# Two pieces of a loaded ahead of b's first slices, in a matmul–GELU–matmul kernel

## The chip, the cores and the metric

The kernel runs on one core of a Trainium2 chip. The metric is the time of one execution on the device in microseconds (us), the median of several runs. Beside it there is one execution taken with the hardware profiler.

## What is computed

```python
m, k, n, p = 1024, 1024, 2048, 1024          # a: m x k, b: k x n, c: n x p, all float32
h = np.matmul(a, b)
h = 0.5 * h * (1 + np.tanh(np.sqrt(2 / np.pi) * (h + 0.044715 * h ** 3)))
return np.matmul(h, c).astype(np.float32)
```

## The kernel before

The order of every engine's instructions is written out by hand, in the order of the program's text; no planner moves anything. TensorE computes h transposed, 128 rows of n at a time ("tiles" t), in two halves h of 512 rows of m. All of it is accumulated in eight PSUM banks of 128 x 512.

The first 512 columns of b (tiles 0 to 3) are done plainly: for each slice k of 128 along the contraction, `block(h, tiles, (k,))` issues one matmul per tile into the bank of that tile, with b's slice (128 x 128 of it) as weights and 512 columns of a transposed, `aT[:, h, k]`, as the moving operand. The rest of b and the whole second matmul are done in the manner of Strassen, as seven products instead of eight (`seven(zero…)`, `seven(one…)`, `seven(two…)`), with sums on VectorE. They come after the plain part and are not touched, but for how one output tile is stored.

a must be transposed, and that too is TensorE's work. It is loaded in eight pieces (h, q): half h, quarter q of the contraction, 512 x 256, 512 KB in float32. A piece is brought to bf16 (`cast_a`, on VectorE and ScalarE) and then turned: `turn(h, q, banks, ab)` is a generator that in each of two steps issues four transposes of 128 x 128 into a PSUM bank and one VectorE copy to `aT`. Each step gives one slice k = 2q + n. The program takes a step with `next(tn)` and puts matmuls between.

Loads come on two queues:

- SP's queue carries float32 pieces, which are then cast on the engines: a(0,0), b's slices 0 and 1 (one load of 512 KB, "b's first pair"), a(1,0), a(0,1), and b's slice 2 (256 KB). They go to `sta` and `stb`, and `cast_b(k, engines…)` splits the cast of one slice of b by columns among the engines named.
- GpSimd's queue carries everything else and casts to bf16 on the way (`abq`, `b1`, `b2`, `c_sb`). It is held back by `gate`, a copy on GpSimd that waits for a(0,0). Its order is a(1,1), b's slice 3, then for q = 2 and 3 a(0,q), b's slices 2q and 2q+1, a(1,q), and after them the rest of b and c. The first eight loads are issued one after the other; each further one waits until the load eight places ahead of it has landed.

`stir(widths…)` issues matmuls of zeros of the given widths, whose result nobody reads; each is a float32 matmul, which the trace shows as two. `make_identity` on GpSimd makes the identity matrix that the transposes multiply with; the first transpose waits for GpSimd, and that includes the gate copy.

The order of TensorE at the head, before the change, is: five stirs of 256; four transposes of a(0,0); stir 128; four transposes of a(0,0); stir 64; `block(0, range(4), (0,))` and `block(0, range(2), (1,))`, six matmuls; the eight transposes of a(1,0); two more matmuls of half 0 and three of half 1; four transposes of a(0,1); three matmuls of half 1; four transposes; and then a loop over q = 1, 2 with blocks of four and three matmuls and four transposes in turn. It ends with a(1,3), the last piece.

In the profile, L114 are the matmuls of `block`, L145 the transposes, L146 the copies to `aT`, L110 the casts on VectorE and L108 those on ScalarE, L125 the stirs, L75 to L79 SP's loads, L81 the gate, L86 and L89 and L92 GpSimd's first loads of a and b, L98 the loads of b's columns 512 to 1023, L212 the matmuls of the seven products, L429 the stores. The changed kernel is four lines shorter, so its numbers are lower by one (L80 to L199) or four (from about L290).

Of the kernel before, what the change touches and what calls it, by code (L numbers as in the profile page):

```python
# [19 lines left out]
def kernel(ctx, tc, a, b, c, out):  # L20
    nc = tc.nc
    M, K = a.shape
    _, N = b.shape
    _, P = c.shape
    H = 512
# [4 lines left out]
    bv = b.rearrange("(kt p) n -> p kt n", p=128)  # L30
# [9 lines left out]
    def slot(tag, shape, dt, name):  # L40
        return big.tile(shape, dt, name=name, tag=tag)

    def bank(i, shape=(128, H), dt=F32, name="ps"):
        return pp.tile(list(shape), dt, name=name, tag=f"bank{i}", padded_shape=None)

    def pieces(tag, bufs, shape, dt, name):
        return small.tile(shape, dt, name=name, tag=tag, bufs=bufs)
# [12 lines left out]
    b1 = slot("b1", [128, KT, 1024], BF16, "b1")  # L60
# [4 lines left out]
    stb = slot("x0", [128, KT, H], F32, "stb")  # L65
    sta = slot("x1", [128, 2, 2, 4, 256], F32, "sta")
    abq = slot("x3", [128, 4, 2, 4, 256], BF16, "abq")

    def a_part(h, q):
        return av[:, 4 * h:4 * h + 4, ds(q * 256, 256)]  # L70

    def b_part(q):
        return bv[:, 2 * q:2 * q + 2, 0:H]

    nc.sync.dma_start(out=sta[:, 0, 0], in_=a_part(0, 0))  # L75
    nc.sync.dma_start(out=stb[:, 0:2], in_=b_part(0))
    nc.sync.dma_start(out=sta[:, 1, 0], in_=a_part(1, 0))
    nc.sync.dma_start(out=sta[:, 0, 1], in_=a_part(0, 1))
    nc.sync.dma_start(out=stb[:, 2], in_=bv[:, 2, 0:H])  # L79

    nc.gpsimd.tensor_copy(gate, sta[:, 0, 0, 3, 0:1])  # L81
    nc.scalar.activation(g, warm[:, 0:1], AF.Gelu_apprx_tanh)
# [2 lines left out]
    def cast_load_a(h, q):  # L85
        nc.gpsimd.dma_start(out=abq[:, q, h], in_=a_part(h, q))  # L86

    def cast_load_b(q):
        nc.gpsimd.dma_start(out=b1[:, 2 * q:2 * q + 2, 0:H], in_=b_part(q))  # L89

    cast_load_a(1, 1)
    nc.gpsimd.dma_start(out=b1[:, 3, 0:H], in_=bv[:, 3, 0:H])  # L92
    for q in range(2, 4):
        cast_load_a(0, q)
        cast_load_b(q)
# [3 lines left out]
    for n in range(2):  # L99
        for k in range(0, KT, 4):  # L100
            nc.gpsimd.dma_start(out=b2[:, k:k + 4, ts(n, H)],
                                in_=bv[:, k:k + 4, ds(1024 + n * H, H)])
# [3 lines left out]
    def copy(eng, dst, src):  # L106
        if eng is nc.scalar:
            nc.scalar.activation(dst, src, AF.Copy)  # L108
        else:
            nc.vector.tensor_copy(dst, src)  # L110

    def mm1(p, t, h, ks):
        for k in ks:
            nc.tensor.matmul(p, b1[:, k, ts(t, 128)], aT[:, h, k],  # L114
                             start=(k == 0), stop=(k == KT - 1))
# [6 lines left out]
    def stir(*widths):  # L122

        for w in widths:
            nc.tensor.matmul(ps[0, 3][:, 0:w], warm[:, 0:128], warm[:, 0:w],  # L125
                             start=True, stop=True, skip_group_check=True)

    def cast_a(h, q, *engs):

        ab = pieces("ab", 2, [128, 4, 256], BF16, "ab")  # L130
        for i, eng in enumerate(engs):
            w = 256 // len(engs)
            for j, e in enumerate(eng if isinstance(eng, tuple) else (eng,)):
                m = slice(2 * j, 2 * j + 2) if isinstance(eng, tuple) else slice(0, 4)
                copy(e, ab[:, m, ts(i, w)], sta[:, h, q][:, m, ts(i, w)])
        return ab

    def turn(h, q, i, ab):

        banks = i if isinstance(i, tuple) else (i,)  # L140
        pts = [bank(x, (128, 2, H), BF16, "pt") for x in banks]
        for n in range(2):
            pt = pts[n % len(pts)]
            for m in range(4):
                nc.tensor.transpose(pt[:, n, ts(m, 128)], ab[:, m, ts(n, 128)], ident)  # L145
            nc.vector.tensor_copy(aT[:, h, 2 * q + n], pt[:, n])  # L146
            yield

    def cast_b(k, *engs):
        c0 = 0  # L150
        for i, eng in enumerate(engs):
            w = (H - c0) if i == len(engs) - 1 else H // len(engs) // 128 * 128
            copy(eng, b1[:, k, ds(c0, w)], stb[:, k, ds(c0, w)])
            c0 += w

    def block(h, tiles, ks):
        for k in ks:
            for t in tiles:
                mm1(ps[h, t], t, h, (k,))
# [56 lines left out]
    def pair(i):  # L216
        x = slot(f"x{i}", [128, 2, 4, H], F32R, "x1")
        return x[:, 0], x[:, 1]
# [8 lines left out]
    one = Seven(4, quarters(b2, 0, H), BB, [None] * 4, zero.t)  # L227

    stir(256, 256, 256, 256, 256)
    tn = turn(0, 0, 4, cast_a(0, 0, nc.vector))  # L230
    next(tn)
    stir(128)
    cast_b(0, nc.vector, nc.vector, nc.scalar)
    next(tn)
    stir(64)
    cast_b(1, nc.scalar)
    ab = cast_a(1, 0, nc.vector, nc.scalar)
    block(0, range(4), (0,))
    block(0, range(2), (1,))
    for _ in turn(1, 0, (7, 6), ab):  # L240
        pass
    block(0, range(2, 4), (1,))
    ab = cast_a(0, 1, (nc.scalar, nc.vector), nc.vector)
    cast_b(2, nc.scalar, nc.scalar)
    for t in range(3):
        ps[1, t] = bank(4 + t)
    zero.t[0], zero.t[1] = pair(2)
    block(1, range(3), (0,))
    tn = turn(0, 1, 7, ab)
    next(tn)  # L250
    block(1, range(3), (1,))
# [2 lines left out]
    for q in range(1, 3):  # L254
        k = 2 * q
        block(0, range(4), (k,))
        tn = turn(1, q, 7, abq[:, q, 1])
# [5 lines left out]
        tn = turn(0, q + 1, 7, abq[:, q + 1, 0])  # L263
# [10 lines left out]
    tn = turn(1, 3, 0, abq[:, 3, 1])  # L274
# [153 lines left out]
    def store(mt, q0, w, ot, eng=None):  # L428
        (eng or nc.sync).dma_start(out=out[ts(mt, 128), ds(q0, w)], in_=ot)  # L429

    def done2(i, l, j, p):
        if (i, l) == (1, 0):
            ot = pieces("o", 4, [128, H], F32, "ot")
            nc.vector.tensor_copy(ot, p)
            p = ot
        n = 2 if (i, l, j) == (0, 0, 1) else 1
        for q in range(n):
            r = ds(q * (H // n), H // n)
            store(4 * i + j, l * H + q * (H // n), H // n, p[:, r])

    def between2(n):
# [12 lines left out]
        elif n == "P73":  # L454
            two.t4(two.t[1], 4)

    seven(two, done2, between2)


# [28 lines left out]
```

## Time and profile before

| | us |
|---|---|
| median of 3 runs | 117.21 (117.09 to 117.56) |
| the profiled execution | 117.6 |
| its span, first to last record | 115.8 |
| TensorE busy with matmuls in the span | 110.7 (96%) |
| VectorE, ScalarE, GpSimd busy | 90.1, 51.4, 17.3 |
| first load issued, first transpose, first matmul of h | 0.74, 5.21, 6.90 |
| last matmul group ends, last VectorE instruction starts | 112.9, 112.93 |

The span is shorter than the execution by 1.8 us, which lie ahead of the first and behind the last record. Lines of a timeline or of a chain begin with the start and the length in us; "x4" means four instructions merged into one line; in square brackets stands how long the engine was idle before it and what ended that. A matmul's own length includes the time until its result is out, so that the next may start before it ends. "To landing" is the time from the start of a load's issue until the last of its parts has arrived.

### The profile page before, as it was taken

Reading aid. Unit: us, or ns where it says so; the run is one execution under the profiler, and the core shown is the slowest. Engines: PE = TensorE matmul, PEld = TensorE weight load, DVE = VectorE, ACT = ScalarE, POOL = GpSimd, SP = SyncE. Lnnn points to the kernel's source line nnn. Section 1 sums busy time; section 2 is a strip of 40 time slices with the busy share of each in tenths; the row PEclk is TensorE's granted clock in tenths of the full one; section 3 lists DMA queues with packets and bytes.
Section 4 is the critical chain, followed back from the end, with each engine's and each line's share of the span. In section 5 each row is a group of like instructions: output and inputs, shape, how many; then the busy total and the mean of one; then the engine's idle time right before and its main releaser. Section 6 shows DMA issues by size and latency. Waiting matters only on the chain.

```text
span 115.8 us, 1473 instructions
## 1 busy us (share of the span) xinstructions
PE 110.7 (96%) x544; PEld 77.1 (67%) x550; DVE 90.1 (78%) x108; ACT 51.4 (44%) x86; POOL 17.3 (15%) x29
## 2 busy tenths in 40 slices
PE   7889999999999999999999999999999999999990
PEld 6545555445777447888886444588888888888870
DVE  0247747689999998944789999999999986964581
ACT  5053000799268998066699339700043992000000
POOL 2497754222332000000000000000000000000000
PEclk9999999999999999999999999999999999999999
DMA  3999999999999999998000000070000002004994
GB/s 74 296 381 221 200 199 204 204 207 207 205 210 210 211 212 212 212 210 163 9 0 0 6 0 0 0 272 0 0 0 0 0 0 94 2 27 173 364 358 166
DMA packets 13414, 15.94 MB, mean 138 GB/s; under 512 B 736, under 2 KB 9184, under 8 KB 13408
## 3 DMA queue, kind: packets, MB, share of 16 engines
q0 software_dynamic: 8672, 9.31, 47.6%
q1 hardware_dynamic: 4592, 6.42, 15.7%
q10 hardware_dynamic: 144, 0.13, 0.3%
q8 instruction: 4, 0.07, 0.2%
q14 instruction: 2, 0.02, 0.0%
HBM read 20.97 MB, written 4.19 MB: 217 GB/s over the span
## 4 chain that ended last, share of the span: by engine, by line
PE 79%; DMA 13%; POOL 5%; issue 0%; DVE 0%
PE ps L212 76%; DMA abq<-in_a_dram 10%; DMA sta<-in_a_dram 3%; POOL abq L86 3%; PE ps L114 2%; POOL b L89 1%; POOL gate L81 1%; PE pt L145 1%; POOL b L92 0%; DVE ot L375 0%
## 5 line engine op out<-in xcount | busy, mean ns | idle before, releaser
L212 PE MATMUL ps<-x,s 128*128 128x512 f32 x128 | 29.6, 391 | 0.0
L212 PEld LDWEIGHTS ps<-x,s 128*128 128x128 f32 x128 | 24.0, 188 | 5.1
L212 PE MATMUL ps<-x,x 128*128 128x512 f32 x96 | 22.9, 394 | 0.0
L212 PEld LDWEIGHTS ps<-x,x 128*128 128x128 f32 x96 | 18.0, 188 | 3.9
L114 PE MATMUL ps<-aT,b 128*128 128x512 bf16 x62 | 15.7, 379 | 0.3 <-DVE b L110 0.2
L298 ACT ACTIVATE v<-ps 128x512 f32<-128x512 f32 x10 | 6.0, 598 | 19.1 <-PE ps L212 19.1
L212 PE MATMUL ps<-c_sb,hT 128*128 128x512 bf16 (+2 forms) x78 | 14.1, 336 | 0.1
L212 PE MATMUL ps<-x 128*128 128x512 f32 x56 | 13.2, 393 | 0.0
L212 PEld LDWEIGHTS ps<-x 128*128 128x128 f32 x56 | 10.2, 188 | 2.7 <-ACT u L298 0.4
L212 PEld LDWEIGHTS <-hT 128*128 128x128 bf16 x80 | 7.1, 98 | 7.0 <-issue 0.5
L118 ACT ACTIVATE hT<-ps 128x512 bf16<-128x512 f32 x14 | 7.3, 596 | 9.6 <-PE ps L114 9.6
L118 ACT ACTIVATE hT<-ot 128x512 bf16<-128x512 f32 x18 | 10.4, 623 | 2.1 <-DVE ot L303 2.0
L146 DVE COPY aT<-pt 128x512 bf16<-128x512 bf16 x16 | 6.7, 422 | 5.5 <-PE pt L145 5.4
L212 PE MATMUL ps<-aT,b 128*128 128x512 bf16 x46 | 10.6, 379 | 0.1
L303 DVE TENSOR_TENSOR ot<-ps,u 128x512 f32<-128x512 f32 x10 | 6.7, 688 | 5.2 <-ACT u L298 5.2
L303 DVE TENSOR_TENSOR ot<-ps,v 128x512 f32<-128x512 f32 x10 | 6.7, 688 | 4.9 <-DMA out_dram<-ot 3.9
L170 DVE TENSOR_TENSOR x<-c_sb 128x1024 fp32r<-128x1024 bf16 x8 | 9.2, 1216 | 0.0
L114 PEld LDWEIGHTS <-b 128*128 128x128 bf16 x64 | 5.7, 97 | 4.5 <-DVE b L110 0.3
L212 PEld LDWEIGHTS <-b 128*128 128x128 bf16 x48 | 4.6, 97 | 5.7 <-issue 0.3
L104 POOL DMA_DIRECT2D c_sb<-in_c_dram x8 | 5.6, 703 | 13.4 <-DMA b<-in_b_dram 11.1
L170 DVE TENSOR_TENSOR x<-b 128x1024 fp32r<-128x1024 bf16 (+1 forms) x4 | 7.0, 1751 | 0.6 <-issue 0.6
L298 ACT ACTIVATE u<-ps 128x512 f32<-128x512 f32 x10 | 5.9, 597 | 3.4 <-PE ps L212 3.2
(44 smaller groups left out, 110.7 us busy)
## 6 DMA issues: line engine op xcount, KB each, us to landing
c_sb<-in_c_dram POOLq DMA_DIRECT2D x8, 512.0 KB, 19.7
out_dram<-ot SPq DMA_DIRECT2D x14, 256.0 KB, 2.1
b<-in_b_dram POOLq DMA_DIRECT2D x6, 512.0 KB, 15.6
sta<-in_a_dram SPq DMA_DIRECT2D x3, 512.0 KB, 6.2
abq<-in_a_dram POOLq DMA_DIRECT2D x5, 256.0 KB, 8.0
stb<-in_b_dram SPq DMA_DIRECT2D x1, 512.0 KB, 5.4
b<-in_b_dram POOLq DMA_DIRECT2D x2, 256.0 KB, 8.3
stb<-in_b_dram SPq DMA_DIRECT2D x1, 256.0 KB, 7.2
```

The source lines that it names most:

```text
L81: nc.gpsimd.tensor_copy(gate, sta[:, 0, 0, 3, 0:1])
L86: nc.gpsimd.dma_start(out=abq[:, q, h], in_=a_part(h, q))
L89: nc.gpsimd.dma_start(out=b1[:, 2 * q:2 * q + 2, 0:H], in_=b_part(q))
L104: nc.gpsimd.dma_start(out=c_sb[:, t:t + 2], in_=cv[:, t:t + 2])
L114: nc.tensor.matmul(p, b1[:, k, ts(t, 128)], aT[:, h, k], start=(k == 0), stop=(k == KT - 1))
L118: nc.scalar.activation(hT[h][:, t], p, AF.Gelu_apprx_tanh)
L145: nc.tensor.transpose(pt[:, n, ts(m, 128)], ab[:, m, ts(n, 128)], ident)
L146: nc.vector.tensor_copy(aT[:, h, 2 * q + n], pt[:, n])
L170: nc.vector.tensor_tensor(out=dst[:, r], in0=x[:, r], in1=y[:, r], op=op)
L212: nc.tensor.matmul(p[:, ds(c0, w)], l[:, k, ts(j, 128)], r[:, k, ds(c0, w)], start=(start and k == 0), stop=(k == self.kt - 1), skip_group ...
L298: nc.scalar.activation(st, p, AF.Copy)
L303: nc.vector.tensor_tensor(out=ot, in0=p, in1=st, op=ADD)
```

## The change

SP's queue loads a(1,0) ahead of b's first pair, and no longer loads b's slice 2. GpSimd's queue loads b's slices 2 and 3 together, in first place, ahead of a(1,1). a(0,0) is cast half on VectorE and half on ScalarE, and its two steps of transposes go to two banks, one straight after the other. After them come the eight transposes of a(1,0), with stirs of 256 and 64 ahead of them and one of 128 behind them, and only then matmuls: four of slice 0 for half 0, three of slice 0 for half 1, four of slice 1 for half 0. These are the same eleven that stood ahead of a(0,1)'s transposes before; from these on the order is the old one. In `cast_b(0, …)` ScalarE takes the first 256 columns as two of 128 and VectorE the last 256 (before, VectorE took the first 256 and ScalarE the last). One more output tile is stored in two halves.

```diff
     nc.sync.dma_start(out=sta[:, 0, 0], in_=a_part(0, 0))
+    nc.sync.dma_start(out=sta[:, 1, 0], in_=a_part(1, 0))
     nc.sync.dma_start(out=stb[:, 0:2], in_=b_part(0))
-    nc.sync.dma_start(out=sta[:, 1, 0], in_=a_part(1, 0))
     nc.sync.dma_start(out=sta[:, 0, 1], in_=a_part(0, 1))
-    nc.sync.dma_start(out=stb[:, 2], in_=bv[:, 2, 0:H])
...
+    cast_load_b(1)
     cast_load_a(1, 1)
-    nc.gpsimd.dma_start(out=b1[:, 3, 0:H], in_=bv[:, 3, 0:H])
...
     stir(256, 256, 256, 256, 256)
-    tn = turn(0, 0, 4, cast_a(0, 0, nc.vector))
-    next(tn)
+    for _ in turn(0, 0, (4, 5), cast_a(0, 0, nc.vector, nc.scalar)):
+        pass
+    stir(256, 64)
+    tn = turn(1, 0, (7, 6), cast_a(1, 0, nc.scalar, nc.vector))
+    next(tn)
+    cast_b(0, nc.scalar, nc.scalar, nc.vector)
+    next(tn)
+    cast_b(1, nc.scalar)
     stir(128)
-    cast_b(0, nc.vector, nc.vector, nc.scalar)
-    next(tn)
-    stir(64)
-    cast_b(1, nc.scalar)
-    ab = cast_a(1, 0, nc.vector, nc.scalar)
-    block(0, range(4), (0,))
-    block(0, range(2), (1,))
-    for _ in turn(1, 0, (7, 6), ab):
-        pass
-    block(0, range(2, 4), (1,))
-    ab = cast_a(0, 1, (nc.scalar, nc.vector), nc.vector)
-    cast_b(2, nc.scalar, nc.scalar)
     for t in range(3):
         ps[1, t] = bank(4 + t)
+    block(0, range(4), (0,))
+    block(1, range(3), (0,))
+    block(0, range(4), (1,))
+    ab = cast_a(0, 1, (nc.scalar, nc.vector), nc.vector)
     zero.t[0], zero.t[1] = pair(2)
-    block(1, range(3), (0,))
     tn = turn(0, 1, 7, ab)
...
-        n = 2 if (i, l, j) == (0, 0, 1) else 1
+        n = 2 if (i, l) == (0, 0) and j else 1
```

## The prediction

> **What bounds the kernel now.** I read the page first: busy shares, then the chain.
>
> ```profile
> PE 110.7 (96%) x544; PEld 77.1 (67%) x550; DVE 90.1 (78%) x108; ACT 51.4 (44%) x86; POOL 17.3 (15%) x29
> ...
> PE ps L212 76%; DMA abq<-in_a_dram 10%; DMA sta<-in_a_dram 3%; POOL abq L86 3%; PE ps L114 2%; POOL b L89 1%; POOL gate L81 1%; PE pt L145 1%; POOL b L92 0%; DVE ot L375 0%
> ```
>
> TensorE is the bound, and 4% of a span of 115.8 is all that is left to it. The change touches the first 11 us only (and one store), so the question is what a shift of TensorE's early work does to its last matmul. The chain in order of time says where TensorE last waited for something from outside:
>
> ```profile
> 10.15 11.43 DMA abq<-in_a_dram
> 21.58 0.05 issue
> 21.63 0.40 PE pt L145 x4
> ```
>
> The last a piece, a(1,3), lands at 21.58; its four transposes start 0.05 later. After that the chain is TensorE's own to 112.93. The timeline of TensorE shows the head:
>
> ```profile
> 5.21 0.40 PE L145 MATMUL pt<-ident,ab 128*128 128x128 bf16 x4 [0.42 <-POOL gate L81]
> ...
> 6.90 1.47 PE L114 MATMUL ps<-aT,b 128*128 128x512 bf16 x6 [0.17 <-DVE b L110]
> 8.47 0.62 PE L145 MATMUL pt<-ident,ab 128*128 128x128 bf16 x8
> 8.93 1.26 PE L114 MATMUL ps<-aT,b 128*128 128x512 bf16 x5
> 10.03 0.39 PE L145 MATMUL pt<-ident,ab 128*128 128x128 bf16 x4
> ...
> 19.16 2.32 PE L114 MATMUL ps<-aT,b 128*128 128x512 bf16 x10
> 21.63 0.40 PE L145 MATMUL pt<-ident,abq 128*128 128x128 bf16 x4
> ```
>
> Ten matmuls take 2.32 with the last one's 0.38, so one follows another after (2.32 - 0.38)/9 = 0.216. The ten end their turn at 19.16 + 10 x 0.216 = 21.32, and the next start is 21.63: TensorE stands idle 0.31 there, for a(1,3). From 10.03 to 21.32 it is full; the windows view gives the same:
>
> ```profile
> 8.40:10.00 1.60, 1.53 (x13) 0.90 (x14) 1.11 (x5) 0.64 (x2) 1.60 (x3) 1.00 1.20 275
> 10.00:21.30 11.30, 11.20 (x80) 6.09 (x81) 7.83 (x16) 1.58 (x4) 6.12 (x9) 1.00 1.35 201
> 21.30:21.70 0.40, 0.26 (x3) 0.08 (x3) 0.22 (x1) 0.40 (x2) 0.00 (x0) 1.00 1.25 205
> 21.70:112.90 91.20, 90.98 (x424) 65.45 (x428) 78.44 (x82) 45.91 (x76) 4.93 (x7) 1.00 0.53 116
> ```
>
> (The first number after each stretch is its length, the next TensorE's busy time, and the 1.00 after the engines is the granted clock.) So two times carry everything: when TensorE reaches the four transposes of a(0,1), at 10.03, with 11 matmuls and 16 transposes behind it; and 21.58. In the changed order the same 11 matmuls and 16 transposes stand ahead of these four transposes, and from there on TensorE's order is the old one. The end moves by (change of 10.03) - 0.31, as long as a(1,3) is no later, and no load between becomes late.
>
> **The change part by part.**
>
> *SP's queue.* Landing times, from issue start plus "to landing" of each load: a(0,0) 0.74 + 3.7 = 4.44; b's pair 1.22 + 5.4 = 6.6; a(1,0) 1.77 + 6.2 = 7.97; a(0,1) 2.27 + 7.1 = 9.4; b's third slice 2.82 + 7.2 = 10.0. They land in the order of issue, so the queue is one pipe: 512 KB took 2.15 (b's pair), then 1.38 and 1.4 (the a pieces). The change swaps second and third. The three first loads are the same bytes, so b's pair now lands when the third load did: 7.97. Ends: if the slowness of the second load (2.15 against 1.38) is gone in the new order, 4.44 + 2 x 1.38 = 7.20; if a(1,0) as the second and b's pair as b each pay it, 4.44 + 2 x 2.15 = 8.74. I take 7.97, because the slowness stays in the sum whether it goes with the place or with the tensor. a(1,0) lands between 5.8 and 6.6. a(0,1) stays at 9.4, and SP issues one load less.
>
> *First matmul.* Before, b's pair landed at 6.6 and the first matmul ran at 6.90, after a 128-wide VectorE cast of 0.22. Now the first 128 columns are ScalarE's. Its casts of b took 0.40 at 256 wide and 0.61 at 512, so 128 wide is about 0.29, and the first matmul comes 0.40 after the landing: 8.37. ScalarE's second 128 (0.2 to 0.29 more) is ready for the second matmul at 8.59; VectorE's 256 columns (0.3) are in time for the third. Slice 1 is one ScalarE cast of 0.61, done by 9.2, and needed at the eighth matmul, 8.37 + 7 x 0.216 = 9.9. The 11 matmuls, now without a gap, end at 8.37 + 11 x 0.216 = 10.74. a(0,1), landed at 9.4, is cast by 9.9 to 10.3 (ScalarE is free at 9.2), so its transposes start at 10.74, against 10.03: **0.71 later**.
>
> *All turns first.* The eight transposes of a(0,0) start together at 5.21 (they wait for the gate copy as before), those of a(1,0) at about 6.5 to 7.3 (landing plus a ScalarE cast of 0.63). They cost nothing: TensorE has no b before 8.3. What the cover costs is the loss itself: before, 6 matmuls (1.3 of TensorE's time) ran between 6.90 and 8.2, while a(1,0) was loading.
>
> *The stir matmuls.* One 256 wide, one 64 and one 128, where 128 and 64 stood. Before, the two took 0.44 and 0.39 with their drain; the new ones end by about 6.2 and 7.9 at the latest, ahead of what they precede. No cost.
>
> *GpSimd's queue.* Eight loads before the first that waits for a slot, as before; b's slices 2 and 3 come as one load in first place, a(1,1) is second. SP's queue is emptied of 256 KB and GpSimd's takes them, so the sum up to a(0,2) and all after it is the same bytes. b's slices 2 and 3 come after 9.4 + 1.3 (the spacing of GpSimd's 512 KB loads) = 10.7, and are needed at 10.74 + 0.22 + 0.65 + 0.22 = 11.8; a(1,1) comes at about 12.0 (before, the loads of both came at 11.3 and 12.0) and is needed at 12.7. Slack 1.1 and 0.7. ScalarE loses a cast of 0.72. Nothing on the path.
>
> Here a rule speaks against the change. The trace: GpSimd's first load, issued at 5.14, took 6.2 to land, 11.34, after the last of SP's queue (10.0), though a(1,0) and a(0,1) still took 1.4 each: GpSimd's bytes did not push SP's back. The Trainium skill, "DMA: Bandwidth & Descriptors", section "Queues, rings and completion order", says that each DMA engine goes round robin between the queues that have work. By that rule b's pair, half loaded when GpSimd's load is queued at 6.0, would share the engines and land up to 1.9 later (an estimate), and the kernel would lose 2.3 instead of 0.4. I go by the row.
>
> *The store.* One 256 KB store at about 75 us becomes two of 128 KB; SP has one load less before. SP's queue waits there for results (100 us in all), and TensorE's chain never passes it before 112.9. No cost; if it were in the way, one issue of 0.5.
>
> **The sum.** +0.71 at a(0,1)'s transposes, -0.31 because a(1,3)'s wait is filled: when TensorE is ready for a(1,3) at 22.03, it has been there since 21.58. End: **+0.40**. The profiled execution took 117.6 (span 115.8), so it would be 118.0; the median of the runs before is 117.21, so the time is **117.6**. That is 0.34%, inside the 0.5% (0.59 us) that a measurement of this kernel can tell from no change.
>
> **The rivals.**
>
> *Nothing is lost* (0.12): b's pair lands by 7.57, the turn comes at most 0.31 late, and a(1,3)'s wait swallows it all. For it: the second load's slowness may lie partly in the start of the queue. 117.2.
>
> *The pipe gets faster* (0.14): the slowness is gone, b's pair lands at 7.20, the transposes of a(0,1) come at 9.97, and every later load is up to 0.77 earlier, so that a(1,3)'s wait goes too: -0.06 - 0.31 = -0.37, 116.85. No more is to be had, since the rest is TensorE's own work; and with the loads where they were, a(1,2) (landed 15.95, its transposes at 16.02) lets TensorE gain nothing at all.
>
> *Slower: b is slow in third place as well, and a(1,0) in second* (0.12): b's pair at 8.74, everything 0.77 later than my sum: +1.17, 118.4. It decides as soon as b's pair lands after 8.16, where the loss passes 0.59.
>
> *Slower: the clock* (0.05). The stirs took 0.43 apart from 2 to 4 us (five starts in the stretch) against 0.22 for a warm pair of the same form. If TensorE's idle stretches (up to 1.1 between 6.2 and 8.3, against 0.4 before) bring back half speed for as long as the first time, 3.3 from 0.78 to 4.04, half of that is lost: +1.6 + 0.4, 119.2. Against it: the clock was 1.00 through all gaps of before, but no gap there was so long.
>
> **How the numbers follow.** The forecast, +0.2 to +0.8, has 0.55, of which 0.15 lies over 0.59; with the two slower rivals that makes 0.32 slower. Faster by over 0.59 needs what no case gives: 0.05, with a bit of the faster pipe. The rest, 0.63, is the same (in it 0.02 that none of these cases names). The range takes in the faster pipe (116.8) and b slow in third place (118.4), and leaves out the clock.
>
> **What would show it.** Right: b's pair lands near 7.97, the first L113 matmul at about 8.4, eleven in a row, the transposes of a(0,1) near 10.74, no gap near 22, the last PE matmul 0.4 later. Wrong: the first matmul before 8.0 or after 8.7; a gap at 11.8 or 12.7 (b's second pair or a(1,1) late); a granted clock under 1; or a new wait for an L97 load (b's next half) near 25 to 27.

## The result and the profile after

The changed kernel takes 118.46 us in the median of seven runs (117.82 to 118.9) against 117.22 (117.09 to 117.56): a ratio of 1.0098, interval 1.007 to 1.0127. (Ratios here and below leave out the few runs that took over about 1.5% longer than the fastest run of their kernel.) The loss has the forecast sign, but the medians differ by 1.24 where the sum had 0.40. The profiled execution took 118.46, its span is 116.7.

The chain of waits after the change, in order of time:

```profile
1.78 6.71 DMA stb<-in_b_dram
8.49 0.02 issue
8.52 0.32 ACT b L107
8.83 0.05 issue
8.88 2.55 PE ps L113 x11
11.43 0.22 PE pt L144 x4
```

The chain no longer goes through GpSimd's queue to a(1,3) at 21.58. It starts at the load of b's first pair, which lands at 1.78 + 6.71 = 8.49, goes through ScalarE's cast of its first 128 columns to the eleven matmuls, and from there stays on TensorE to 113.77 (before: 112.91). a(1,0) had landed at 5.57, as ScalarE's cast of it shows:

```profile
5.59 0.63 ACT L107 ACTIVATE ab<-sta 128x512 bf16<-128x512 f32 x1 [0.70 <-DMA sta<-in_a_dram]
```

The timeline of TensorE:

```profile
6.96 0.76 PE L144 MATMUL pt<-ident,ab 128*128 128x128 bf16 x8
7.55 0.44 PE L124 MATMUL ps<-const-float32-0.0 128*128 128x128 f32 x2
8.88 2.55 PE L113 MATMUL ps<-aT,b 128*128 128x512 bf16 x11 [0.89 <-ACT b L107]
11.27 0.39 PE L144 MATMUL pt<-ident,ab 128*128 128x128 bf16 x4
...
20.40 2.32 PE L113 MATMUL ps<-aT,b 128*128 128x512 bf16 x10
22.56 0.39 PE L144 MATMUL pt<-ident,abq 128*128 128x128 bf16 x4
```

Both turns are over by 7.7 and TensorE stands idle 0.89, waiting for b. The transposes of a(0,1) begin at 11.27 instead of 10.03, 1.24 later. At 20.40 + 10 x 0.216 = 22.56 a(1,3)'s transposes follow without a gap: the 0.31 of idle time that stood there is filled. From a(1,3)'s transposes to the last matmul both traces take the same to within 0.07, and the last matmul ends 0.86 later than before.

By the prediction's own signs the sum was wrong in one point: the first matmul came at 8.88, and "after 8.7" was named as a sign of being wrong. The other signs are those of "right": eleven matmuls in a row, no gap near 22, no lower clock ahead of the last matmul.

The waits of TensorE's weight loads show no DMA any more (before: 0.9 for `abq`); in the head only this wait for another engine is left:

```profile
PEld L113 <- ACT b L107: 1.1, 1, 1.1
```

### The profile page after: what moved, and what is told of

It reads as the page before. It is cut to its first block, busy times and chain, and to the rows that moved or that the text cites. A ratio compares the mean times of both kernels' runs of the same rounds, so it can differ in the third digit from the quotient of the medians.

```text
span 116.7 us, 1481 instructions
## 1 busy us (share of the span) xinstructions
PE 112.1 (96%) x552; PEld 78.5 (67%) x552; DVE 90.1 (77%) x107; ACT 51.4 (44%) x86; POOL 17.2 (15%) x29
## 4 chain that ended last, share of the span: by engine, by line
PE 90%; DMA 6%; SPq 1%; ACT 0%; DVE 0%; issue 0%
PE ps L211 75%; PE ps L113 12%; DMA stb<-in_b_dram 6%; PE pt L144 3%; SPq L76 0%; SPq L75 0%; ACT b L107 0%; DVE ot L371 0%
```

## The experiments

All ratios are against runs of the kernel before on the same chip, at 117.25 to 117.38 in the median. Three theories are compared: **late b** (the end is set by the landing of b's first pair, plus eleven matmuls), **GpSimd's queue** (its earlier and larger first load takes DMA time from b's pair), and **clock** (TensorE loses its full clock for want of early work).

**The changed kernel again.** No edit.

> The changed kernel once more, nothing edited. Theory 'late b' (the end is set by the landing of b's first pair plus eleven matmuls; in the first trace it landed at 8.49, not at 7.97): 118.2 to 118.7, b's pair landing at 8.2 to 8.7, its time varying with that landing. Rival 'GpSimd's queue' (its first load, now larger and earlier, takes DMA time from b's pair): the same time, and the first packets of that load ahead of b's landing. Rival 'clock' (TensorE is granted full speed late, because less work is packed before 8): the same time too, with the clock granted after 6.

Measured: 118.7 (117.71 to 119.11), ratio 1.0103 (1.007 to 1.0136). The profiled execution took 119.11, and in it b's pair landed later still. From its chain:

```profile
1.78 7.32 DMA stb<-in_b_dram
9.48 2.55 PE ps L113 x11
```

The landing is 9.10, 0.61 later than in the first trace; the time is 0.65 longer. So the landing isn't one number. GpSimd's first data moved at 8.11, ahead of the landing, as "GpSimd's queue" had it too; the next run tells the two apart. If the time follows it in the other runs as it does in these two, the six runs, 117.71 to 119.11, had the pair land between 7.7 and 9.1 (an estimate: the time less the 110.0 that lie between landing and end in both traces).

**SP's loads alone.**

```diff
 # against the kernel before
     nc.sync.dma_start(out=sta[:, 0, 0], in_=a_part(0, 0))
+    nc.sync.dma_start(out=sta[:, 1, 0], in_=a_part(1, 0))
     nc.sync.dma_start(out=stb[:, 0:2], in_=b_part(0))
-    nc.sync.dma_start(out=sta[:, 1, 0], in_=a_part(1, 0))
```

> The kernel before with a(1,0) ahead of b's first pair on SP's queue, and nothing else: TensorE's order, GpSimd's queue and the store are the old ones. Late b: b's pair at 8.0 to 8.5, first matmul 0.3 later, then eleven matmuls and eight transposes (2.4 + 0.45) without a gap, so a(0,1)'s transposes at 11.2 to 11.7 against 10.03 and the end 0.9 to 1.4 later: 118.1 to 118.6. GpSimd's queue: b's pair at 8.0 or earlier, since GpSimd's loads are the old ones, 117.6 to 118.1. Clock: TensorE's early work is the old one in length but comes later, no clear number.

Measured: 121.3 (120.18 to 122.75), ratio 1.0318 (1.0282 to 1.0354), worse than any theory had it. b's pair landed at 1.78 + 7.39 = 9.17 with GpSimd's queue as it was, so GpSimd's new order is not what makes the pair late; in this trace's DMA records GpSimd's first data moved at 8.91, 0.26 ahead of that landing. What was missed is the clock, in the windows view:

```profile
6.76:10.18 3.42, 0.98 (x7) 0.58 (x6) 0.98 (x4) 0.99 (x3) 3.42 (x6) 1.00 1.10 309
10.18:13.59 3.41, 3.41 (x15) 1.76 (x14) 1.61 (x5) 1.60 (x4) 1.52 (x3) 0.50 1.36 206
```

After a stretch of 3.4 with 0.98 of TensorE work the granted clock is 0.50 for the next 3.4. The mean clock is 0.972 to 0.986 in all six runs; in the thirteen runs of the changed kernel it is 0.996 to 1.000. So with the new load order the changed kernel's order of TensorE, turns and stirs together, keeps the clock, and the old order does not.

**TensorE's order alone.**

```diff
 # against the changed kernel: SP's first three loads as before the change, and
     stir(256, 64)
+    cast_b(0, nc.scalar, nc.scalar, nc.vector)
+    cast_b(1, nc.scalar)
     tn = turn(1, 0, (7, 6), cast_a(1, 0, nc.scalar, nc.vector))
     next(tn)
-    cast_b(0, nc.scalar, nc.scalar, nc.vector)
     next(tn)
-    cast_b(1, nc.scalar)
```

> The changed kernel with the old order of SP's loads (b's first pair second, a(1,0) third), and the casts of b's slices 0 and 1 ahead of a(1,0)'s; all turns still come first. Late b: it is not b that counts here but a(1,0), at 8.0: its cast takes 0.65 and its transposes 0.45, then eleven matmuls, 2.4: a(0,1)'s transposes at 11.5, the end 1.1 later than before, 118.3. So the new order of TensorE would cost about as much with the old loads. GpSimd's queue: a(1,0) as third load late as b was, 8.5, 118.8. Clock: 118 to 119 with the full clock after 6.

Measured: 119.19 (118.97 to 120.48), ratio 1.0182 (1.014 to 1.0224). b's pair landed at 6.6 and a(1,0) at 7.94, the old values to within 0.03; a(1,0)'s transposes ran at 8.65, behind 2.46 of idle time. Here too the clock fell in two of six runs, the profiled one among them (0.50 from 8.05 to 11.47), which the expectation did not have. The other four took 118.97 to 119.33, more than the 118.3 of "late b"; why isn't shown, as the only trace has the lower clock. Each half of the change alone costs more than both: the old order of loads and the old order of turns go together, as do the new ones. (The second of these two kernels has GpSimd's new order too.) The old pair hides six matmuls behind a(1,0)'s landing, the new one has nothing to hide behind b's.

**GpSimd's part and the store alone.**

```diff
 # against the kernel before
-    nc.sync.dma_start(out=stb[:, 2], in_=bv[:, 2, 0:H])
...
+    cast_load_b(1)
     cast_load_a(1, 1)
-    nc.gpsimd.dma_start(out=b1[:, 3, 0:H], in_=bv[:, 3, 0:H])
...
-    cast_b(2, nc.scalar, nc.scalar)
...
-        n = 2 if (i, l, j) == (0, 0, 1) else 1
+        n = 2 if (i, l) == (0, 0) and j else 1
```

> The kernel before with GpSimd's part and the store alone: b's slices 2 and 3 as one load first on GpSimd's queue, no load and no cast of slice 2 on SP's, and the second output tile stored in two halves as well. Late b: nothing on the path, 117.1 to 117.4. GpSimd's queue: a(1,0) and a(0,1) land later by 0.3 or more, 117.6 to 118.2. Clock: 117.2.

Measured: 117.94 (117.35 to 118.36), ratio 1.0041 (1.0016 to 1.0066), against an expected nothing. SP's loads landed as before (a(1,0) at 7.91, a(0,1) at 9.3), so in this trace it did not go the way of "GpSimd's queue". The trace is of the fastest run, 117.35, and gives only a hint: a(1,1), now second on GpSimd's queue, landed at 12.04, and its transposes waited for it until 12.09, where TensorE was ready at about 12.0:

```profile
PEld L144 <- DMA abq<-in_a_dram: 0.7, 2, 0.5
```

There is no slack left there when TensorE keeps its old schedule. That the slower runs had a(1,1) later is not shown. In the changed kernel a(1,1) landed at 12.50 and was needed at 13.25, so this cost lies hidden behind b's lateness.

**b's pair in fourth place.**

```diff
 # against the changed kernel
-    nc.sync.dma_start(out=stb[:, 0:2], in_=b_part(0))
     nc.sync.dma_start(out=sta[:, 0, 1], in_=a_part(0, 1))
+    nc.sync.dma_start(out=stb[:, 0:2], in_=b_part(0))
```

> The changed kernel with b's first pair one place later still on SP's queue, behind a(0,1). Late b: the pair lands 1.0 to 1.8 later than the 8.5 to 9.1 it had in third place, at 9.8 to 10.6, and the end follows it one to one: 119.7 to 120.5, unless the clock falls in the longer idle time of TensorE (from about 8 to 10.5), which would add up to 1.7. If the end were set by something else (GpSimd's loads, the turns), it would stay at 118.5.

Measured: 119.03 (118.51 to 120.98), ratio 1.0131 (1.0103 to 1.0159), less than expected, because the pair did not land where I had put it: at 2.31 + 6.74 = 9.05, 1.43 after a(0,1). Here b's pair was as fast as a piece of a, and a(0,1), ahead of it in third place, took 1.98 (5.64 to 7.62) instead of 1.4. The profiled execution took 119.0, again the pair's landing plus 110 (the table below has all such traces). In one of the four runs, 120.98, the clock fell (mean 0.986).

**An early read of b.** In this and the next, the first thing on ScalarE's queue is a small read into a tile that nobody uses.

```diff
 # against the changed kernel; room is an unused [128, 16] float32 tile
+    nc.scalar.dma_start(out=room.rearrange("p (k o) -> p k o", k=2), in_=bv[:, 0:2, 0:8])
     nc.sync.dma_start(out=sta[:, 0, 0], in_=a_part(0, 0))
```

> The changed kernel, and ScalarE's queue reads, as the first thing it does, the first 32 bytes of each of the 256 row pieces of b's first pair into an unused tile. Two theories of why b's pair is slow on SP's queue (2.15 in second place, 2.9 to 3.4 in third, where a's pieces take 1.4). 'First touch' (the first reads of b are slow, wherever they stand): the pair lands 0.7 to 1.5 earlier, at 7.3 to 7.8, and the time falls to 117.2 to 117.8. 'Shape or place' (reads of 2 KB, or what runs beside them): the pair lands at 8.4 to 9.2 as before, 118.4 to 118.9.

Measured: 118.55 (118.29 to 118.75), ratio 1.0105 (1.0085 to 1.0126): the time of "shape or place", but with the landing of "first touch". b's pair landed at 7.34, 1.34 after a(1,0), as fast as a piece of a. The first matmul came at 7.72 and a(0,1)'s transposes at 10.11, nearly the old 10.03. Then another wait took its place:

```profile
5.90 6.79 DMA abq<-in_a_dram
12.74 0.40 PE pt L145 x4
```

a(1,1), second on GpSimd's queue, landed at 5.90 + 6.79 = 12.69, and its transposes ran at 12.74 instead of 12.02. GpSimd's first load, b's slices 2 and 3, now had the slow stretch that b's pair had been spared: packets of it took up to 1.0 in the trace's DMA records between 8 and 9, where 0.1 is usual. Of the 118.39 of this execution 0.4 belongs to the early read itself: 3.3 lie between the start of the last VectorE instruction and the end of the span, against 2.9, with one load more ahead of the last stores. In the kernels below that have the early read but one store less it is 2.9 again; why the count matters isn't shown.

**The same in the kernel before.**

> The same early read of b in the kernel before. First touch: b's pair lands at 5.9 instead of 6.6 and all loads behind it come 0.7 earlier; TensorE's first matmul at 6.2, the eleven matmuls done at about 9.3 to 9.5, and the wait for a(1,3) is gone or shorter: 116.4 to 116.9. Shape or place: 117.2 to 117.5.

Measured: 117.77 (117.48 to 118.25), ratio 1.0045 (1.0029 to 1.0062). The early read had landed only at 4.25, 0.6 after the first packet of b's pair (3.66); the pair landed at 6.65, as without it. The last matmul ends within 0.05 of where it did in the profiled execution of before; the same 0.4 behind it is the loss of this execution.

**b's pair in narrow rows.**

```diff
 # against the changed kernel
-    nc.sync.dma_start(out=stb[:, 0:2], in_=b_part(0))
+    for c in range(2):
+        nc.sync.dma_start(out=stb[:, 0:2, ts(c, 256)], in_=bv[:, 0:2, ts(c, 256)])
```

> The changed kernel with b's first pair loaded as two halves by columns, so that one row piece is 1 KB as in a's loads. Shape: b's halves take 0.7 each like a's pieces, the second lands at 7.2 to 7.5, the time is 117.2 to 117.6. First touch, or place: the second half lands at 8.4 to 9.2, 118.4 to 119.0 (one issue of 0.5 more on SP, ahead of its data by more than that).

Measured: 118.78 (118.58 to 118.94), ratio 1.0124 (1.0102 to 1.0146). The second half landed at 2.31 + 6.39 = 8.70, 3.0 after a(1,0), with rows of 1 KB. So the size of the row pieces is not the reason.

**Without the stirs behind the first turn.** `stir(256, 64)` and `stir(128)` are left out of the changed kernel.

> The changed kernel without the stirs of 256 and 64 and of 128 behind the first turns (the five at the start stay). Late b: the stirs fill idle time only, 118.4 to 118.8, unless the clock falls. Clock: TensorE has only 0.9 of transposes between 5 and 8.5, the granted clock falls to a half for one stretch of 3.4 in most runs and the mean clock to 0.985; half of what of that stretch holds work is lost, 119.5 to 120.5.

Measured: 119.47 (118.92 to 120.71), ratio 1.0197 (1.0151 to 1.0243). In two of four runs the mean clock was 0.985 and 0.986, and these took 119.78 and 120.71; the other two 118.92 and 119.17. This lies between the two expectations: where the clock held, leaving out the stirs cost little (118.92 and 119.17, against 117.71 to 119.11 in the runs of the changed kernel), and in two of four runs it cost the clock.

**An early read of all of b**, 32 bytes of every eighth row; the third output tile is stored whole again, so that as many loads and stores precede the last stores as in the changed kernel.

```diff
 # against the changed kernel
+    nc.scalar.dma_start(out=room[:, 0:8], in_=b.rearrange("(p s) n -> p s n", s=8)[:, 0, 0:8])
...
-        n = 2 if (i, l) == (0, 0) and j else 1
+        n = 2 if (i, l, j) == (0, 0, 1) else 1
```

> The changed kernel with an early read on ScalarE's queue that touches all of b: 32 bytes of every eighth row, 128 in all, into an unused tile. The third output tile is stored whole again, so that as many loads and stores precede the last stores as in the changed kernel (the earlier early read moved these by one, and 0.45 more lay behind the last matmul). First touch: b's pair lands at 7.3 to 7.5 and GpSimd's first load (b's slices 2 and 3) is not slow either, so a(1,1) lands at 11.3 to 11.6 and TensorE does not wait for it: 117.2 to 117.5. If the slow stretch has to do with when and beside what b is read, the pair or GpSimd's first load is slow again: 117.9 to 118.7.

Measured: 118.75 (118.33 to 120.93), ratio 1.0116 (1.0095 to 1.0137). The read was over at 2.9, and b's pair still landed at 9.26, slow as ever. So "first touch", as I had it, by stretches of 64 KB, is wrong. What helped above was a read of each row that the pair would read. In two of the eight runs, 120.93 (the profiled one) and 120.87, the clock fell; in the stretch ahead of that TensorE had been busy half the time.

**The same with b's slices one by one.**

```diff
 # against the last one; both output tiles are stored whole
-    nc.sync.dma_start(out=stb[:, 0:2], in_=b_part(0))
+    nc.sync.dma_start(out=stb[:, 0], in_=bv[:, 0, 0:H])
+    nc.sync.dma_start(out=stb[:, 1], in_=bv[:, 1, 0:H])
```

> As the last one, and b's first pair is loaded as two loads of one slice each, still behind a(1,0); both output tiles are stored whole. First touch: slice 0 lands at 6.7, its seven matmuls start at 7.1, slice 1 at 7.4 in time for the other four; a(0,1)'s transposes start at 9.4 to 9.6 against 10.03, and b's and a's later loads are 0.6 earlier than before: 116.6 to 117.0, better than both kernels. If a stretch of b's loads is slow in any case: 117.5 to 118.3.

Measured: 118.79 (118.42 to 118.94), ratio 1.012 (1.0101 to 1.0138). Slice 0 landed at 7.84 and the first seven matmuls ran at 8.23, but slice 1 came at 9.47 and the other four at 10.18. a(0,1), behind them in the queue, landed only at 10.83, and its transposes ran at 11.40. This was meant to beat both kernels and does not.

**The early read of all of b in the kernel before.** The second output tile is stored whole.

> The kernel before with the same early read of all of b; the second output tile is stored whole. First touch: b's pair lands at 5.9 to 6.3, the loads behind it 0.3 to 0.7 earlier, 116.6 to 117.0. If the early read takes longer than b's pair waits for its turn (from about 3.6), nothing changes: 117.2 to 117.5.

Measured: 117.52 (117.13 to 118.01), ratio 1.001 (0.9989 to 1.0032). No change. The read was over at 3.5, b's pair landed at 6.87 all the same, and no run points to a version better than the kernel before.

## Why the loss was two to three times the forecast

**The structure of the sum held.** Eleven matmuls without a gap took 11.27 - 8.88 = 2.39 (2.37 in the sum), the first followed its landing by 0.39 (0.40), the gap near 22 is gone, GpSimd's loads were in time with the slack that was given (a(1,1) 0.75 ahead, 0.7 in the sum), the store cost nothing visible, and in thirteen runs of the changed kernel the clock never fell. The "two" is from the profiled executions (0.86 between the last matmuls), the "three" from the medians (1.24). In five traces, all those with the full clock in which TensorE's order is the new one and the pair's landing sets its start, the time of the execution is that landing plus 110.0:

| kernel | b's pair lands | execution | difference |
|---|---|---|---|
| changed | 8.49 | 118.46 | 109.97 |
| changed, again | 9.10 | 119.11 | 110.01 |
| b fourth | 9.05 | 119.00 | 109.95 |
| b narrow | 8.70 | 118.67 | 109.97 |
| without stirs | 8.98 | 118.92 | 109.94 |

With the 7.97 of the prediction that line gives 117.97, the 118.0 that the prediction named for the profiled execution. So for the profiled execution it was one term.

**The term that was mis-sized: b's landing.** The step says that "the slowness stays in the sum whether it goes with the place or with the tensor". The sum did not stay: the second and the third load together took 2.15 + 1.38 = 3.53 before, and 1.33 + 2.92 = 4.25 and 1.47 + 3.26 = 4.73 in the two traces of the changed kernel. The slowness went with b's pair from second to third place, and it grew; in fourth place it was on the load ahead (1.98) and not on the pair (1.43), so it is not simply a property of b's load either. The prediction's rival "b is slow in third place as well, and a(1,0) in second" named about the right time, 118.4, in part by luck: a(1,0) was not slow, and at the rival's landing, 8.74, the line above gives 118.7. Nothing in the trace of before showed b in third place; to name bounds (7.20 to 8.74) was the right step, and the middle was taken with too much trust. The second trace, at 9.10, is outside of them.

**A second term: the wait for a(1,3).** In the profiled execution of before there was such a wait to be filled, and the last matmuls of the two profiled executions are 0.86 apart: 1.24 less the 0.31 of idle time and the 0.07 lost behind it. But the medians differ by 1.24. The trace of before is of the slowest of its seven runs, 117.56, 0.34 above their median. In it fifteen of the sixteen parts of a(1,3) had landed by 19.92 and the last came at 21.58; a transfer of 16 KB of instructions ran at 19.57 for 0.97, and that it held up this part is a guess, since the records don't name the DMA engine. The kernel with GpSimd's part alone and the kernel before with either early read keep the old order of TensorE, and none of their three traces has such a gap. In order of the experiments:

```profile
19.25 2.32 PE L113 MATMUL ps<-aT,b 128*128 128x512 bf16 x10
21.41 0.39 PE L144 MATMUL pt<-ident,abq 128*128 128x128 bf16 x4
```

```profile
19.48 2.32 PE L115 MATMUL ps<-aT,b 128*128 128x512 bf16 x10
21.64 0.39 PE L146 MATMUL pt<-ident,abq 128*128 128x128 bf16 x4
```

```profile
19.67 2.32 PE L115 MATMUL ps<-aT,b 128*128 128x512 bf16 x10
21.83 0.39 PE L146 MATMUL pt<-ident,abq 128*128 128x128 bf16 x4
```

a(1,3) had landed at 19.95, 20.25 and 20.38 there. If most runs of the kernel before are like these, there is nothing to fill and the loss is the whole 1.24; and 117.56 less 0.38 is 117.18, close to the median of 117.22. That fits, but there is only one trace of the kernel before itself, so it is argued and not shown. The sum was made against one execution and its wait was taken for all of them.

**The rule on DMA queues.** The rule of the Trainium skill's "DMA: Bandwidth & Descriptors" ("Queues, rings and completion order"), round robin between queues, would have had b's pair late because of GpSimd's load. The pair was late, but equally so with GpSimd's old queue (9.17). The DMA records of the changed kernel show GpSimd's first data at 7.77, 2.3 after the issue had ended and 0.36 before the first part of a(0,1), the last of SP's loads, landed (8.12). In all fourteen traces these two times are 0.30 to 0.36 apart, though the first runs from 7.54 to 8.95: GpSimd's load began when the first part of SP's last load was nearly through. For GpSimd's queue measurement and rule differ here again.

**What stays open** is why b's pair is slow. It is neither the row size (8.70 with 1 KB) nor GpSimd's queue, and a read of every eighth row does not help, but one of every row does, in the one trace there is of that. There the next b load, whose rows had not been read, was slow. But rows that nobody has read are not enough to make a load slow: in the changed kernel itself GpSimd's load of b's slices 2 and 3, also unread, landed 1.30 after a(0,1), and in the DMA records every packet of it took 0.10. Nor does the cost stay with b's own packets, as the pair in fourth place shows.

## What to carry to other kernels

A load whose pace differs from its neighbours' must not be priced by the place in the queue: keep both ends, and when one landing decides the loss, give the bad end its full weight. Here it turned out worse than the bad end in one of two traces. Work that hides a load counts as much as the load: here a new order of loads with the old order of turns, and the reverse, each cost more than both new orders together. And a wait that a sum means to fill should be looked for in more than one execution, at least in how far the profiled one lies from the median.

## What the runs showed that I had not expected

The clock falls for less idle time than I had thought. When it falls in the head, it stays at 0.50 for 3.41, and whether it falls goes with TensorE's time in the 3.41 ahead of that. The Trainium skill, in "TensorE: Matmul & The Clock Gate" ("The HAM clock gate"), gives its window the same length. But the window need not be idle to lose the clock: it fell after windows with 0.98, 1.55 and 1.70 of TensorE time in 3.41, and held after windows with 1.66, 1.78 and 1.84. So about half busy is the edge; it isn't sharp in this measure, since 1.70 lost the clock and 1.66 kept it. Windows that lost it, with the one that follows, from the kernel with the early read of all of b and from that with TensorE's order alone:

```profile
6.39:9.80 3.41, 1.70 (x15) 1.22 (x14) 1.80 (x5) 0.52 (x3) 3.41 (x5) 1.00 1.08 282
9.80:13.21 3.41, 3.41 (x9) 1.29 (x9) 0.73 (x3) 0.92 (x2) 1.61 (x3) 0.50 1.39 202
```

```profile
4.64:8.05 3.41, 1.55 (x14) 1.19 (x13) 1.38 (x5) 1.35 (x5) 3.41 (x6) 1.00 1.03 323
8.05:11.47 3.42, 2.82 (x14) 1.91 (x15) 2.24 (x5) 0.96 (x2) 2.60 (x4) 0.50 1.27 217
```

Windows that kept it, from the kernel without the stirs and from the changed kernel run again:

```profile
4.40:7.81 3.41, 1.66 (x19) 1.06 (x17) 2.12 (x5) 1.19 (x2) 3.41 (x6) 1.00 0.88 237
7.81:11.22 3.41, 1.86 (x9) 0.91 (x10) 1.47 (x4) 1.45 (x4) 2.93 (x4) 1.00 1.21 260
```

```profile
6.59:10.00 3.41, 1.78 (x17) 1.34 (x16) 1.72 (x5) 0.88 (x3) 3.41 (x5) 1.00 1.11 280
```

Where the windows lie differs from execution to execution: by the traces' clock records, full clock was first granted at 4.04 in the trace of before, at 6.57 in the first of the changed kernel, and at 4.40 without the stirs. That is a likely reason why the same kernel loses the clock in some runs only; the runs without a trace don't show it.

In its second trace the changed kernel is near that edge. With b a little later it might have paid the clock too, some 2 us, as the 120.93 of the kernel with the early read of all of b did against its 118.33 to 119.07.
